# A decoder layer on one core: two left operands of the down projection's first group split in the feed-forward, and one set of copies given to ScalarE

## The chip, the core and the metric

The kernel runs on one core of a Trainium2 chip. The metric is device time in microseconds for one launch, median of three runs. All arithmetic is float32; a large matrix product is made of reduced-precision passes on TensorE, as told below.

## What is computed

One layer of a decoder with 1024 tokens and a model width of 1024. The change lies in the feed-forward (width 2816) and in its down projection; mixing and output projection stand ahead of them, a gated embedding and a last norm behind.

```python
h = rms_norm(x, mix_norm_g[i])
z = h @ w_in[i]
...
x = x + jnp.concatenate([y_nsa, y_conv, y_gla], axis=-1) @ w_out[i]
h = rms_norm(x, ffn_norm_g[i])
x = x + (jax.nn.silu(h @ ffn_w_gate[i]) * (h @ ffn_w_up[i])) @ ffn_w_down[i]
gate = jax.nn.sigmoid(rms_norm(x, ple_norm_g[i]) @ ple_w_gate[i])
x = x + (p[i] @ ple_w_proj[i]) * gate
...
return rms_norm(x, final_norm_g)
```

## The kernel before

**Split operands.** A float32 matrix enters TensorE as two halves: `split` lets ScalarE cast it to the reduced type (the high half, line 1040) and lets VectorE or GpSimd subtract that from the original (the low half, line 267). Each product then takes three matmuls: high by high, low by high, high by low. A split tile is named `op`; it has 128 partitions and two halves of 512 columns (512 KiB).

**Seven products for eight.** Gate, up and down projections are made of 2 by 2 blocks by a Strassen-Winograd scheme: seven block products and a number of block sums. The sums lie on VectorE and GpSimd.

**The feed-forward** walks over 11 pairs of hidden tiles, `c` = 0 to 10. A pair's gate and up weights (`w_g`, `w_u`) are loaded and split, multiplied (lines 1051 to 1053), and drained by `quarters`. The activation leaves in four blocks a11, a21, a12, a22, held in two tiles `sg`. Already here the block sums that the down projection will want as left operands are made: s5 = a21 + a22 and s6 = s5 - a11 in the tile `sa` (lines 1318 and 267), s3 in `ws`, and a21 = a11 - a21. All seven left operands go to device memory in `actd[c]`, unsplit, by SyncE's queue (lines 1322 to 1326).

**The down projection** takes the pairs in four groups (`DOWN`): 0, 1, 2, then 3, 4, 5, then 6, 7, 8, then 9, 10. A group makes its seven products in the order 5, 6, 3, 1, 7, 4, 2, each over all its pairs. `Down` loads a pair's two weight tiles (`w_d`, line 1355), left operands 5 and 6 (one load of 512 KiB from `actd`, line 1365) and operand 2 (`st`, line 1360). `operands(n)` loads the later left operands two at a time (3 and 1; 7 and 4), makes the right operand's block sum on VectorE and splits both sides. The matmuls are line 1436: 4 row tiles by 3 pairs by 3 passes, 36 for a product of the first group, about 924 in all. `drain` adds each finished bank to the residual `x2` (line 1345), which has come back from device memory as `x1d` (line 1421); product 1 of the first group is copied to the tile `xp` instead (line 1399).

**What sets the order.** The program is recorded once to plan SBUF: each tile is given one of 50 slots, and a tile waits until the last user of its slot's former tile is done (a DMA that reads that tile is such a user). Then a scheduler orders the instructions of each engine; each engine takes them strictly in that order. SyncE's queue issues all the loads and stores spoken of here, in order too, so a load stands behind any store ahead of it. There, the first group's loads and splits are mixed with the last feed-forward pair's work.

## Time and profile before

| | |
|---|---|
| median of three runs | 1401.75 us (1401.25 to 1402.43) |
| the profiled execution, its own time | 1404.31 us |
| its span, first to last instruction | 1402.5 us |
| TensorE busy (matmuls) | 1373.9 us, 98% |
| VectorE, ScalarE, GpSimd busy | 1030.6, 658.9, 554.5 us |
| feed-forward, lines 1051 to 1053 | from 638 to 1066 us of the span |
| down projection, line 1436 | from 1049.5 to 1280 us |

The span is what the trace shows; the profiled execution's own time lies 1.8 us above it. TensorE's share is an average: what an edit is worth is read where TensorE waits. In a row of the timeline a bracket gives how long the engine was idle just before, and what ended that. "SPq" is SyncE issuing a DMA; the transfer itself runs on.

### The profile page before, as it was taken

The numbers are of one execution on the slowest core, as the hardware profiler recorded it, in microseconds if no ns is written. First come the engines' busy times: TensorE is split into PE (matmuls) and PEld (weight loads), VectorE is DVE, ScalarE is ACT, GpSimd is POOL, SyncE is SP. The second block draws the span as 40 slices with busy tenths as digits, with TensorE's granted clock in tenths as the row PEclk, the third lists the DMA queues.
The fourth block names the chain that finished last, engine by engine and source line by source line (L and its number), as shares of the span: only waits on it lengthen the run. The fifth ranks groups of instructions, "written<-read, shape, count | busy, mean of one in ns | idle before, by whom it ended". The sixth has DMA issues, their size and how long they took to land.

```text
span 1402.5 us, 19415 instructions
## 1 busy us (share of the span) xinstructions
PE 1373.9 (98%) x7080; PEld 1163.3 (83%) x7080; DVE 1030.6 (73%) x1870; ACT 658.9 (47%) x1286; POOL 554.5 (40%) x592
## 2 busy tenths in 40 slices
PE   8999999999999998999999999999999999999997
PEld 6898777889999987888878888888888788888886
DVE  3897557558998885658786777777689989897533
ACT  7331422247887885536433334333345344444532
POOL 3761444347887863101465566556510000000111
PEclk9999999999999999999999999999999999999999
DMA  9201013400000012441333222233356743521111
GB/s 361 75 16 40 11 54 102 153 17 5 5 9 5 5 61 89 170 150 46 113 113 109 84 87 105 98 113 113 113 212 242 256 147 116 176 79 65 69 40 46
DMA packets 55743, 135.68 MB, mean 97 GB/s; under 512 B 5412, under 2 KB 10206, under 8 KB 55646
## 3 DMA queue, kind: packets, MB, share of 16 engines
q1 hardware_dynamic: 55502, 134.42, 27.5%
q8 instruction: 55, 0.90, 0.3%
q14 instruction: 42, 0.34, 0.1%
q10 hardware_dynamic: 144, 0.01, 0.0%
HBM read 102.68 MB, written 31.73 MB: 96 GB/s over the span
## 4 chain that ended last, share of the span: by engine, by line
PE 87%; DVE 6%; DMA 3%; ACT 1%; POOL 1%; issue 1%; SPq 0%; POOLq 0%; DVEq 0%; ACTq 0%
PE banks L1436 13%; PE banks L1053 8%; PE banks L1052 8%; PE banks L1051 8%; PE banks L371 3%; PE banks L967 3%; PE banks L368 3%; PE banks L372 3%; PE banks L1011 2%; PE banks L1012 2%; PE banks L907 2%; PE banks L1152 2%; PE banks L1153 2%; PE banks L1154 2%; PE banks L1488 2%; PE banks L1486 2%
## 5 line engine op out<-in xcount | busy, mean ns | idle before, releaser
L1053 PE MATMUL banks<-op 128*128 128x512 f32 x616 | 237.8, 390 | 1.3 <-DVE op L267 1.3
L1052 PE MATMUL banks<-op 128*128 128x512 f32 x616 | 238.6, 390 | 0.0
L1051 PE MATMUL banks<-op 128*128 128x512 f32 x616 | 235.9, 390 | 0.3 <-ACT cp L1126 0.3
L1436 PE MATMUL banks<-op 128*128 128x512 f32 x924 | 212.8, 392 | 3.3 <-ACT op L1040 2.6
L1436 PEld LDWEIGHTS banks<-op 128*128 128x128 f32 x924 | 174.3, 189 | 41.0 <-ACT op L1040 3.4
L1040 ACT CAST op<-nat 128x512 fp32r<-128x512 f32 x200 | 118.9, 620 | 177.8 <-DVE op L267 58.8
L267 DVE TENSOR_TENSOR op<-nat,op 128x512 fp32r<-128x512 f32 x196 | 152.5, 799 | 29.6 <-ACT op L1040 29.4
L301 POOL TENSOR_SCALAR rsr<-ss 128x1 f32<-128x1 f32 x16 | 5.9, 368 | 342.2 <-ACT sq L1455 264.4
L1053 PEld LDWEIGHTS banks<-op 128*128 128x128 f32 x616 | 115.6, 188 | 26.4 <-DVE op L267 2.2
L1051 PEld LDWEIGHTS banks<-op 128*128 128x128 f32 x616 | 115.6, 188 | 25.1 <-ACT cp L1126 0.7
L1052 PEld LDWEIGHTS banks<-op 128*128 128x128 f32 x616 | 115.6, 188 | 24.3 <-issue 0.5
L267 DVE TENSOR_TENSOR op<-ws,op 128x512 fp32r<-128x512 f32 x88 | 87.9, 1002 | 52.5 <-ACT op L1040 52.4
L922 POOL TENSOR_SCALAR p<-p,sums,gates 128x640 f32<-128x640 f32 (+7 forms) x128 | 100.4, 795 | 37.1 <-DVE sums L918 27.5
L913 ACT ACTIVATE p<-p,mn 128x640 f32<-128x640 f32 (+7 forms) x128 | 94.7, 742 | 10.2 <-DVE mn L910 10.1
L368 PE MATMUL banks<-hT,whi 128*128 128x512 f32 x208 | 84.2, 406 | 6.8 <-ACT hT L324 6.2
L1040 ACT CAST op<-ws 128x512 fp32r<-128x512 f32 x88 | 54.4, 622 | 76.9 <-PE banks L1053 45.6
L371 PE MATMUL banks<-hT,whi 128*128 128x512 f32 x208 | 83.7, 402 | 0.5 <-DVE hT L325 0.5
L372 PE MATMUL banks<-hT,wlo 128*128 128x512 f32 x208 | 82.5, 398 | 0.0
L967 PE MATMUL banks<-cst,p 128*128 128x128 f32 x448 | 71.8, 276 | 2.2 <-DVE pt L267 1.2
L907 PE MATMUL banks<-k,qst 128*128 128x512 f32 (+2 forms) x192 | 68.3, 362 | 1.4 <-POOL qst L267 0.9
L267 DVE TENSOR_TENSOR pt<-banks,pt 128x512 fp32r<-128x512 f32 (+1 forms) x114 | 64.2, 570 | 6.3 <-ACT pt L978 5.3
L1345 DVE TENSOR_TENSOR x<-banks,x 128x512 f32<-128x512 f32 x96 | 64.1, 681 | 6.4 <-PE banks L1436 6.0
(306 smaller groups left out, 3306.2 us busy)
## 6 DMA issues: line engine op xcount, KB each, us to landing
nat<-actd SPq DMA_DIRECT2D x33, 512.0 KB, 5.6
nat<-in_w_g SPq DMA_DIRECT2D x22, 512.0 KB, 3.3
nat<-in_w_u SPq DMA_DIRECT2D x22, 512.0 KB, 3.2
nat<-in_w_d SPq DMA_DIRECT2D x22, 512.0 KB, 5.3
nat<-in_w_t SPq DMA_DIRECT2D x13, 512.0 KB, 4.1
actd<-sg SPq DMA_DIRECT2D x22, 256.0 KB, 2.4
actd<-sa SPq DMA_DIRECT2D x11, 512.0 KB, 2.8
actd<-sg SPq DMA_DIRECT2D x11, 512.0 KB, 3.7
```

The lines of the kernel that those rows point to most:

```text
L267: return eng.tensor_tensor(out=o, in0=i0, in1=i1, op=ALU.subtract)
L368: r = mm(o, hi[:, w], x[:, 0, :], start=kt == 0, stop=False)
L371: mm(o, hi[:, w], x[:, 1, :], start=False, stop=False)
L372: mm(o, lo_[:, w], x[:, 0, :], start=False, stop=kt == KT - 1)
L907: mark("pe", mm(ps[:, :max(w, 256)], q, kdup[br][g][:, k], start=True, stop=False))
L922: nc.gpsimd.tensor_scalar(out=ps_out[br][:, :n], in0=ps_out[br][:, :n], scalar1=sums[:, br:br + 1], scalar2=gates[:, qb, 3 * head(h) + 1 + ...
L967: nc.tensor.transpose(ps[:, (2 * m + e) * P:(2 * m + e + 1) * P], blk(e, kb, br, ka), ident)
L1040: nc.scalar.copy(o[:, 0, :], src)
L1051: mm(ps, w[:, 0, c], x[k][:, 0, :], start=start and k == 0, stop=False, skip_group_check=True)
L1052: mm(ps, w[:, 0, c], x[k][:, 1, :], start=False, stop=False, skip_group_check=True)
L1053: mm(ps, w[:, 1, c], x[k][:, 0, :], start=False, stop=k == 3, skip_group_check=True)
L1436: mm(groups[g][t], r[:, v, c], l[:, u, :], start=start and (i, u, v) == (0, 0, 0), stop=i == len(ops) - 1 and u == 1, skip_group_check=True)
```

## The change

Three things change. For the pairs of the first group (`c` in 0, 1, 2) the feed-forward splits s5 and s6 as soon as they are made, and stores the two split tiles in a new device array `acts` (two stores of 512 KiB where one of 512 KiB was). The down projection's first group loads those split tiles ready for TensorE (two loads of 512 KiB where one was), and so neither casts nor subtracts for the left side of products 5 and 6. And the first group's product 1 is copied from its banks by ScalarE, not VectorE.

```diff
+    acts = dram.tile([len(DOWN[0]), 2, P, 2, 512], F32, name="acts")
...
-                nc.sync.dma_start(out=actd[c, 0:2].rearrange("i p j -> p i j"), in_=sa)
+                if c in DOWN[0]:
+                    for i, x in enumerate((s5, s6)):
+                        nc.sync.dma_start(out=acts[c, i], in_=f(split(x)))
+                else:
+                    nc.sync.dma_start(out=actd[c, 0:2].rearrange("i p j -> p i j"), in_=sa)
...
-            self.load(5, 6)
+            self.cut = {}
+            if c in DOWN[0]:
+                for i in range(2):
+                    self.cut[5 + i] = B("op", F32R, (P, 2, 512))
+                    nc.sync.dma_start(out=f(self.cut[5 + i]), in_=acts[c, i])
+            else:
+                self.load(5, 6)
...
-            return split(x.a.pop(n)), split({3: x.b22, 1: x.b11, 7: x.b12, 2: x.b21}.get(n, x.t))
+            return x.cut.pop(n) if n in x.cut else split(x.a.pop(n)), split({3: x.b22, 1: x.b11, 7: x.b12, 2: x.b21}.get(n, x.t))
...
-                nc.vector.tensor_copy(p, o)
+                nc.scalar.copy(p, o)
```

The slots and the scheduler's order move with it, from the first pair of the feed-forward on. Three places matter below. A tile's number differs between the two programs.

VectorE, where the feed-forward's last sums (`ws`, `sa`) meet the first group's operands, before: `op_9722` and `op_9730` are the left sides of product 3 for the group's second and third pair, `op_9733` is the third pair's right side, and `ws_9512` is the last pair's s3.

```order
L267 TENSOR_TENSOR ws_9512<-sg_9454,sa_9524 128x512
L267 TENSOR_TENSOR op_9956<-st_9540,op_9956 128x512
L267 TENSOR_TENSOR op_9722<-nat_9567,op_9722 128x512
L267 TENSOR_TENSOR op_9730<-nat_9576,op_9730 128x512
L267 TENSOR_TENSOR op_9959<-nat_9536,op_9959 128x512
L267 TENSOR_TENSOR op_9962<-st_9548,op_9962 128x512
L267 TENSOR_TENSOR op_9965<-nat_9544,op_9965 128x512
L267 TENSOR_TENSOR op_9733<-nat_9552,op_9733 128x512
```

And now, where `op_9740` is the third pair's left side of product 3 (the other sides of product 3 stand further ahead) and `ws_9534` is the last pair's s3:

```order
L267 TENSOR_TENSOR op_9845<-nat_9722,op_9845 128x512
L1350 TENSOR_TENSOR x2_9616<-banks_67,x2_9616 128x512
L1350 TENSOR_TENSOR x2_9617<-banks_67,x2_9617 128x512
L267 TENSOR_TENSOR op_9740<-nat_9598,op_9740 128x512
L267 TENSOR_TENSOR ws_9534<-sg_9476,sa_9546 128x512
L1350 TENSOR_TENSOR x2_9618<-banks_67,x2_9618 128x512
```

Counted from the tenth pair's s5 (`sa` from `sg`), the last piece of product 3 was VectorE's 103rd instruction and is now its 82nd: six low halves fewer stand ahead of it, and the scheduler has put others behind it. On TensorE the first matmul that needs that piece was the 184th after the first of line 1436 and is now the 147th.

SyncE, at the same time, before: `nat_9712`, `nat_9720` and `nat_9728` are the loads of left operands 7 and 4 for the three pairs.

```order
L1365 DMA nat_9712<-actd_2367 128x2x512
L1325 DMA actd_2367<-sg_9454 128x512
L1365 DMA nat_9720<-actd_2367 128x2x512
L1322 DMA actd_2367<-sa_9524 128x2x512
L1324 DMA actd_2367<-sg_9453 128x2x512
L1326 DMA actd_2367<-sg_9454 128x512
L1355 DMA nat_10014<-in_w_d 128x1024
L1355 DMA nat_10022<-in_w_d 128x1024
L1365 DMA nat_10056<-actd_2367 128x2x512
L1323 DMA actd_2367<-ws_9512 128x512
L1365 DMA nat_9728<-actd_2367 128x2x512
```

And now, where the same three are `nat_9722`, `nat_9730` and `nat_9738`:

```order
L1376 DMA nat_9722<-actd_2367 128x2x512
L1376 DMA nat_9730<-actd_2367 128x2x512
L1330 DMA actd_2367<-sg_9476 128x512
L1376 DMA nat_9738<-actd_2367 128x2x512
L1331 DMA actd_2367<-sg_9476 128x512
L1327 DMA actd_2367<-sa_9546 128x2x512
L1329 DMA actd_2367<-sg_9475 128x2x512
L1360 DMA nat_10024<-in_w_d 128x1024
L1328 DMA actd_2367<-ws_9534 128x512
```

The third load stood behind the store of the last pair's s3 (`ws`); now it stands ahead of four of the five stores.

ScalarE, at the end of the feed-forward's first pair, now (the waits are in brackets; `op_6768` and `op_6772` are the split s5 and s6, `op_6914` is the first weight operand of the next pair's up product):

```order
L1040 CAST op_6768<-sa_6763 128x512 [waits DVE_49]
L1040 CAST op_6772<-sa_6763 128x512 [waits DVE_49]
L1040 CAST op_6868<-ws_6812 128x512 [waits Pool_49]
L1116 COPY cp_6836<-banks_67 128x512 [waits PE_49]
L1040 CAST op_6930<-nat_6747 128x512 [waits DMAHW0_49,Activation_49]
L1040 CAST op_6850<-ws_6812 128x512 [waits DVE_49]
L1040 CAST op_6914<-nat_6747 128x512 [waits DMAHW5_49,Activation_49]
```

The first two casts are new. `op_6914` takes the slot of `op_6768`, so its cast waits for that tile's store; before, the same operand's cast waited for the store of `sa`. TensorE wants it at the 238th matmul of the feed-forward, before at the 250th.

## Rows read from the trace of the kernel before

**Rows 1.** The page, busy time by engine: busy us, share of the span, instructions.

```profile
PE 1373.9 (98%) x7080; PEld 1163.3 (83%) x7080; DVE 1030.6 (73%) x1870; ACT 658.9 (47%) x1286; POOL 554.5 (40%) x592
```

**Rows 2.** Stretches of 20 us: busy us (count) by engine, clock, DMA share, GB/s.

```profile
core 0: us, PE busy (x) PEld busy (x) DVE busy (x) ACT busy (x) POOL busy (x), PEclk, DMA share, GB/s
...
1060.00:1080.00 20.00, 20.00 (x90) 16.57 (x89) 19.76 (x34) 10.65 (x20) 0.00 (x0) 1.00 0.57 196
1080.00:1100.00 20.00, 16.67 (x68) 12.71 (x67) 19.52 (x33) 9.69 (x18) 0.00 (x0) 0.95 0.78 282
1100.00:1120.00 20.00, 20.00 (x87) 16.47 (x86) 18.74 (x32) 8.26 (x15) 0.00 (x0) 0.96 0.60 216
```

**Rows 3.** Timeline of TensorE, start of the down projection (start us, us, idle before).

```profile
1049.53 0.84 PE L1436 MATMUL banks<-op 128*128 128x512 f32 x3
...
1066.08 16.48 PE L1436 MATMUL banks<-op 128*128 128x512 f32 x72
1083.33 9.15 PE L1436 MATMUL banks<-op 128*128 128x512 f32 x39 [0.78 <-ACT op L1040]
1093.27 2.10 PE L1436 MATMUL banks<-op 128*128 128x512 f32 x8 [0.78 <-DVE op L267]
1097.14 13.02 PE L1436 MATMUL banks<-op 128*128 128x512 f32 x49 [1.77 <-ACT op L1040]
```

**Rows 4.** Short stretches of TensorE alone: busy us, clock, DMA.

```profile
1098.00:1100.00 2.00, 2.00 (x7) 0.53 1.04 410
1100.00:1104.00 4.00, 4.00 (x16) 0.81 0.89 331
```

**Rows 5.** Timeline of VectorE over the same time.

```profile
1029.01 0.69 DVE L1318 TENSOR_TENSOR sa<-sg 128x512 f32<-128x512 f32 x1
...
1070.89 0.68 DVE L1345 TENSOR_TENSOR x<-banks,x 128x512 f32<-128x512 f32 x1
...
1091.93 1.88 DVE L267 TENSOR_TENSOR op<-nat,op 128x512 fp32r<-128x512 f32 x3
```

**Rows 6.** Timelines of SyncE's issues and of ScalarE.

```profile
1050.85 12.11 SPq L1421 DMA_DIRECT2D x<-x1d  x16
...
1076.40 0.37 SPq L1365 DMA_DIRECT2D nat<-actd  x1
...
1089.81 0.42 SPq L1323 DMA_DIRECT2D actd<-ws  x1
1090.32 0.39 SPq L1365 DMA_DIRECT2D nat<-actd  x1
...
1096.47 1.14 ACT L1040 CAST op<-nat 128x512 fp32r<-128x512 f32 x2 [3.04 <-DMA nat<-actd]
```

**Rows 7.** DMA rate from 1020 to 1120 us, in 40 slices of 2.5 us.

```profile
GB/s 0 3 0 105 7 298 345 307 395 413 402 388 396 391 387 386 387 388 308 272 2 0 2 207 332 193 134 264 123 392 414 405 391 146 0 51 359 327 211 243
```

**Rows 8.** Feed-forward's first pairs: TensorE's waits, a cast, landings of the `sa` store.

```profile
704.16 0.50 PE L1053 MATMUL banks<-op 128*128 128x512 f32 x1 [0.78 <-DVE op L267]
...
711.96 0.50 PE L1051 MATMUL banks<-op 128*128 128x512 f32 x1 [0.26 <-ACT cp L1126]
...
734.31 0.50 PE L1053 MATMUL banks<-op 128*128 128x512 f32 x1 [0.52 <-DVE op L267]
...
696.79 0.62 ACT L1040 CAST op<-nat 128x512 fp32r<-128x512 f32 x1 [8.08 <-DMA actd<-sa]
...
DMA to landing us min/median/max: 2.8/2.8/6.6
```

**Rows 9.** A stretch of 20 us there, columns as in rows 2.

```profile
700.00:720.00 20.00, 18.97 (x82) 14.92 (x81) 17.57 (x18) 8.94 (x15) 13.89 (x10) 1.00 0.15 54
```

**Rows 10.** Groups by line and shape: busy us, mean ns (the last from 600 to 740).

```profile
L1040 ACT CAST op<-nat 128x512 fp32r<-128x512 f32 x117 | 68.2, 619 | 80.7 <-PE banks L1436 40.4 <-DVE op L267 19.3 <-DMA nat<-actd 10.8
...
L1399 DVE COPY xp<-banks 128x512 f32<-128x512 f32 x4 | 2.6, 678 | 0.0
...
L1095 ACT COPY cp<-banks 128x512 f32<-128x512 f32 x3 | 1.7, 580 | 7.7 <-PE banks L1053 7.7
...
L267 DVE TENSOR_TENSOR op<-nat,op 128x512 fp32r<-128x512 f32 x19 | 17.8, 953 | 6.6 <-ACT op L1040 6.5
```

## Prediction

> **What bounds the kernel now.** I read the busy times first: TensorE is at 98% of the span [rows 1], so an edit elsewhere can only give back time in which TensorE stands or runs slowly. Next I read its list of waits and the same engine over stretches. In the feed-forward's steady part and from 1120 us on it never stands. Around the change it stands in two places: three times in the first group of the down projection [rows 3], and three times briefly in the feed-forward's first pairs [rows 8].
>
> The first place is the dear one. Idle time there is 0.78 + 0.78 + 1.77 = 3.33 us [rows 3], and behind it the granted clock is 0.53 for 2 us and 0.81 for 4 us [rows 4]; before, the clock was full [rows 2]. Undisturbed matmuls start (16.48 - 0.39) / 71 = 0.2266 us apart (0.39 us being one matmul, 72 of them in the row) [rows 3]. The two disturbed stretches hold 68 and 87 matmuls where an undisturbed one holds 90, that is 25 too few [rows 2], and 25 by 0.2266 is 5.7 us. Clock and idle time alone give 3.33 + 2 x 0.47 + 4 x 0.19 = 5.0 us. So 5.0 to 5.7 us lie there, and I take 5.6.
>
> Why does it stand? VectorE is busy 19.5 to 19.8 us of each 20 there [rows 2], with one instruction of 128x512 every 0.602 us (three take 1.88 us with the last one's 0.68) [rows 5]. It is a backlog: the last pair's sums and the first group's low halves share one queue. Count it. The last low half of product 3 is instruction 103 after the sum at 1029.01 us; 103 x 0.602 is 62.0 us, so 1091.0 us, and with some waits on the way it is the second in the row of 1091.93 us, ready at about 1093.2 [rows 5]. TensorE would want it at 1049.53 + 184 x 0.2266 = 1091.2 us [rows 3]: 2 us late, the first two waits. The third wait has another cause: a cast at 1096.47 us waited for a load issued at 1090.32 us, right behind the store of `ws` at 1089.81 us [rows 6], which needs VectorE's sum of the last pair. That is the backlog again, by way of SyncE's order.
>
> **The change, part by part.** *Work taken from the crowded stretch.* Six casts and six low halves go. On ScalarE, busy about half of that time [rows 2], six casts of 0.62 us are worth nothing by themselves. On VectorE six instructions are 3.6 us. With the new order, the last piece of product 3 is instruction 82: 1029.01 + 82 x 0.602 = 1078.4 us, with 1 us of waits as now and its own 0.68 ready at 1080.1. TensorE wants it at 1049.53 + 147 x 0.2266 = 1082.8 us. From 2 us late it becomes 2.7 us early. The last operand of product 7 was wanted 192 matmuls in, at 1093.0 us, and came at 1097.1 [rows 3]; it is now wanted 222 in, at 1099.8 us, as VectorE's instruction 106, ready at about 1094.5. Its load no longer stands behind the store of `ws`, and its slot comes free 63 instructions in, at 1067 to 1068 us; behind the residual's loads it should land before 1080. I credit the whole 5.6 us and then charge what follows.
>
> *Loads added.* Three more loads of 512 KiB, 1.57 MB, enter a stretch in which DMA runs at 386 to 413 GB/s from 1040 to 1065 us [rows 7]: 4.0 us of transfer. Everything behind them is up to 4.0 us later. The residual's sixteen loads, last issued at 1050.85 + 12.11 = 1063 us [rows 6] and moved by about 1068 [rows 7], then end at about 1072. The first drains, at 1070.89 us now [rows 5], need only the earlier ten of them, 1.5 MB sooner, so by about 1068; the rest are wanted by product 6's drains, some 80 instructions in, at about 1077. The third pair's weights are wanted by VectorE 44 instructions in, 1055.5 us, and may come 0.5 to 1.5 us after that. That wait eats into the 2.7 us margin. Bounds: 0 (inside the margin) and 4.0 - 2.7 = 1.3 us with a fall of the clock as now, 1.7 us, so 3.0. I charge 0.5, since the margin is nearer to covering it.
>
> *Product 1's copies.* Four instructions of 0.68 us leave VectorE and four of 0.58 us enter ScalarE [rows 10]. Before, they lie at about 1105 us, where TensorE runs at work in hand [rows 2]; product 2, which adds to the same banks, starts 20 matmuls or 4.5 us after product 1 ends. Cost and gain nothing, unless ScalarE stands then (second rival).
>
> *Splits added to the feed-forward.* At the end of pairs 0, 1 and 2, two casts of 0.62 us and two low halves of about 0.95 us (that is their mean there, beside GpSimd's work) [rows 10]. ScalarE is busy 8.9 and VectorE 17.6 of 20 us in the fullest stretch [rows 9]; over a pair's 38 us there is room. From both sides: the 1.56 us that TensorE stands there now could vanish, or all six low halves could be exposed, 6 x 0.95 = 5.7 us. I take 0, nearer the first, as VectorE has idle time in every such stretch.
>
> *The store that holds a slot.* Now the next pair's operand waits for the store of `sa`; its cast starts at 696.79 us after 8.08 us of idle ScalarE, and the low halves behind it are late by the 0.78 us at 704.16 [rows 8]. After the change the operand waits for the store of split s5 and is wanted 12 matmuls earlier, 2.7 us. TensorE's want was about 697.5 us (the cast just met it); it becomes 694.8. With an issue at about 690 us and landings of 2.8 to 6.6 us [rows 8], the cast would end between 693.4 and 697.2: 1.4 us early to 2.4 late. I take 0, since the median landing of the eleven stores is 2.8 us, the least of them. The Trainium skill, in "DMA: Bandwidth & Descriptors", section "Anatomy of one DMA", speaks against splitting into more stores: each DMA has a fixed part of about 2 us, most of it the receipt of the write, plus its bytes by 436 GB/s. For 512 KiB that is an estimate of 3.2 us a store by that page, fitted to another engine's DMAs; with it the cast would end 1.0 us early and the charge stays 0, while the slowest landing of the trace would cost 2.4 us a pair.
>
> Sum: -5.6 + 0.5 + 0 + 0 = -5.1 us. Of the profiled execution's 1404.31 us that makes 1399.2; it was 2.6 us longer than the median of 1401.75, and against that median the forecast is **1396.6 us**.
>
> **The rivals.** *Second: the hole moves.* For it speaks the DMA rate, at its ceiling already [rows 7], and that ScalarE's new order puts a cast for the next group, whose load must wait for a slot until about 1094 us, ahead of the third pair's left operand of product 2, which TensorE wants 246 matmuls in, at 1105.3 us. Against it: either has about 3 us of room. If the 4.0 us appear in full, 3.0 us come back in place of 0.5: 1401.75 - 5.6 + 3.0 = 1399.2; with worse landings up to 1401.
>
> *Third: no effect.* If the waits come from SyncE's queue and the slots alone and not from VectorE's backlog, the loads land as late as now: 1401.5 us. For it speaks the third wait, which ended with a DMA [rows 6]; against it, that the store ahead of that load waited for VectorE.
>
> *Fourth: slower.* The stores of split tiles hold slots in the first three pairs. At the slowest landing, 2.4 us a pair is 7.2 us, and one fall of the clock adds 1.7: 1401.75 - 5.1 + 8.9 = 1405.5 us. It decides from (5.1 + 2.8 - 1.7) / 3 = 2.1 us a pair. For it: TensorE already stands three times just there [rows 8]. Against: 2.8 us is the median landing, and 6.6 us the worst [rows 8].
>
> **How the numbers follow.** The likeliest case has 0.66; its own range is 1394.5 (5.7 us back and the 1.56 us too) to 1398.5. The second has 0.16, the third 0.10, the fourth 0.08. Beyond 0.2% of 1401.75, 2.8 us, a measurement of this kernel tells a change from none. All of the first and some 0.06 of the second lie below 1398.9: faster 0.72. Same is 0.10 of the second and the third, 0.20; slower 0.08. For 8 in 10 the range runs from 1394.5 to 1401.0, which takes in the second case and leaves out the third and fourth.
>
> **What would show it.** Right: TensorE's three waits of rows 3 are gone or under 0.5 us in sum, the stretches up to 40 us behind the first line 1436 matmul (now 1447) hold 90 matmuls each at full clock, and the feed-forward's first pairs wait no more than 1.6 us in all. Loads added: the residual's loads end about 4 us later with VectorE short of a drain for 1 us at most. Wrong: a wait of TensorE on a cast or low half near 1080 to 1105 us with a clock below 1 behind it (second), the third load of operands 7 and 4 still issued near 1090 us (third), or waits of 2 us and more near 695, 735 and 773 us that end with a cast held by a DMA from `acts` (fourth).

## Result and the profile after

The changed kernel takes **1418.2 us** (median of five runs, 1414.5 to 1422.0) against 1402.4 us for the kernel before (1401.3 to 1407.9): a ratio of 1.011, 95% interval 1.0089 to 1.013. It is 1.1% slower where 0.4% faster was forecast, and far outside the range.

The profiled execution took 1419.36 us, its span 1417.6 us. The page's busy times, which answer to [rows 1], hardly move: TensorE 5 us more, VectorE 6 us more.

```profile
PE 1379.2 (97%) x7080; PEld 1164.3 (82%) x7080; DVE 1036.8 (73%) x1866; ACT 662.7 (47%) x1290; POOL 554.9 (39%) x592
```

The loss is found by stages. The summary of TensorE's lines gives the first and last start of a line's matmuls: 1051 is the feed-forward's first pass, 1447 (before: 1436) the down projection. First the kernel before, then the changed one:

```profile
L1051 PE MATMUL banks<-op x616: 387/389/799, 638.0 to 1065.4; 128*128 128x512 f32 x154
...
L1436 PE MATMUL banks<-op x924: 387/389/628, 1049.5 to 1279.8; 128*128 128x512 f32 x185
```

```profile
L1051 PE MATMUL banks<-op x616: 387/389/799, 640.0 to 1083.5; 128*128 128x512 f32 x154
...
L1447 PE MATMUL banks<-op x924: 387/389/502, 1067.9 to 1295.4; 128*128 128x512 f32 x185
```

From the first matmul of the feed-forward to the first of the down projection it is 1067.9 - 640.0 = 427.9 us; before, 1049.5 - 638.0 = 411.5. From there to the end of the last one of the down projection (0.4 us long) it is 227.9 us; before, 230.7. So in this profile 2.8 us came back where 5.6 were credited, and 16.4 us were lost where nothing was expected. Below these two lengths are called the feed-forward and the down projection. (The 2 us ahead of 640 us are not read as an effect of the change: in the runs below that keep the 46 slots the first matmul of the feed-forward lies anywhere from 633.5 to 642.1 us.)

Stretches of 20 us, columns as in [rows 2]:

```profile
680.00:700.00 20.00, 19.06 (x85) 15.34 (x84) 19.16 (x27) 8.05 (x14) 9.50 (x5) 1.00 0.47 169
...
740.00:760.00 20.00, 16.93 (x67) 13.76 (x68) 10.89 (x14) 8.60 (x14) 6.52 (x6) 0.91 0.24 89
...
780.00:800.00 20.00, 15.80 (x63) 12.51 (x62) 13.50 (x15) 7.22 (x12) 9.93 (x7) 0.91 0.40 143
1080.00:1100.00 20.00, 20.00 (x90) 16.57 (x89) 20.00 (x35) 10.68 (x20) 0.00 (x0) 1.00 0.88 320
1100.00:1120.00 20.00, 18.51 (x81) 14.69 (x81) 18.44 (x31) 7.67 (x14) 0.00 (x0) 1.00 0.76 281
```

Two feed-forward stretches hold 67 and 63 matmuls of 90, and none of the engines beside TensorE is full there. In the whole feed-forward TensorE now stands 12.7 us in eight waits, before 1.6 us in three. Its longest waits there, and in the first group of the down projection:

```profile
743.07 0.50 PE L1051 MATMUL banks<-op 128*128 128x512 f32 x1 [3.92 <-ACT op L1040]
...
788.32 0.50 PE L1051 MATMUL banks<-op 128*128 128x512 f32 x1 [4.20 <-ACT op L1040]
...
1110.31 16.87 PE L1447 MATMUL banks<-op 128*128 128x512 f32 x72 [1.49 <-ACT op L1040]
1127.89 12.31 PE L1447 MATMUL banks<-op 128*128 128x512 f32 x53 [0.71 <-DVE x L1350]
```

The last two answer to [rows 3]: 2.2 us in place of 3.33, and the clock behind them stays at 1.00. The first two, 8.1 of the 12.7 us, are new. Who was late? ScalarE's timeline at the first of them:

```profile
734.31 0.59 ACT L1126 COPY cp<-banks 128x512 f32<-128x512 f32 x1
740.93 1.06 ACT L1308 ACTIVATE sg<-sg 128x1024 f32<-128x1024 f32 x1 [6.03 <-DVE sg L1272]
741.90 0.60 ACT L1040 CAST op<-ws 128x512 fp32r<-128x512 f32 x1
742.40 0.61 ACT L1040 CAST op<-nat 128x512 fp32r<-128x512 f32 x1
```

ScalarE stood 6 us in front of a Silu of the next pair's gate; the cast that TensorE wants is queued behind it. The Silu waits for VectorE, where the pair's sums and the split's two low halves (`op<-sa`) stand ahead of the gate's quarters (lines 1271 and 1272):

```profile
734.56 0.68 DVE L267 TENSOR_TENSOR op<-sa,op 128x512 fp32r<-128x512 f32 x1
735.16 1.77 DVE L267 TENSOR_TENSOR ws<-sg,sa 128x512 f32<-128x512 f32 x1
736.85 0.68 DVE L267 TENSOR_TENSOR op<-nat,op 128x512 fp32r<-128x512 f32 x1
737.46 1.77 DVE L267 TENSOR_TENSOR op<-sa,op 128x512 fp32r<-128x512 f32 x1
739.15 0.68 DVE L1271 TENSOR_TENSOR sg<-banks,cp 128x512 f32<-128x512 f32 x1
739.86 1.04 DVE L1272 TENSOR_TENSOR sg<-sg,rbc 128x512 f32<-128x512 f32 x1
```

And on GpSimd the sum behind the wanted cast (`ws<-nat`, line 1105) was itself late, by 0.87 us for a slot that a store still read; it was done at 738.68 us, 3.2 us ahead of its cast:

```profile
729.40 1.68 POOL L1314 TENSOR_TENSOR sg<-cp,sg 128x512 f32<-128x512 f32 x1 [0.63 <-DVE cp L1272]
734.98 1.41 POOL L1136 TENSOR_TENSOR cp<-cp 128x512 f32<-128x512 f32 x1 [3.90 <-ACT cp L1126]
737.26 1.42 POOL L1105 TENSOR_TENSOR ws<-nat 128x512 f32<-128x512 f32 x1 [0.87 <-DMA actd<-sg]
```

Before, GpSimd did the same pair's two products of gate and up (line 1313) together, at 721.74 us, and had the next sum at 730.70:

```profile
721.74 2.93 POOL L1313 TENSOR_TENSOR sg<-cp,sg 128x512 f32<-128x512 f32 x2 [0.63 <-DVE cp L1271]
729.01 1.29 POOL L1136 TENSOR_TENSOR cp<-cp 128x512 f32<-128x512 f32 x1 [4.34 <-ACT cp L1126]
730.70 1.30 POOL L1105 TENSOR_TENSOR ws<-nat 128x512 f32<-128x512 f32 x1 [0.39 <-PE banks L1053]
```

So the second product ended 4.4 us later than before (731.08 against 724.67, less the 2 us of the start), since the scheduler had moved it behind other work. The theories to part: **work** (twelve casts and low halves in the way), **stores** (a second store of 512 KiB a pair, and slots held until it lands; the prediction's fourth rival), **order** (of the engines' queues), and, as none of the first three explained all of it, **slots** (each split tile takes one of the 46 slots of 4 KiB per partition).

### The profile page after: what moved, and what is told of

Read it like the earlier page. It is cut to its first block, busy times and chain, and to the rows that moved or that the text cites. A ratio compares the mean times of both kernels' runs of the same rounds, so it can differ in the third digit from the quotient of the medians.

```text
span 1417.6 us, 19465 instructions
## 1 busy us (share of the span) xinstructions
PE 1379.2 (97%) x7080; PEld 1164.3 (82%) x7080; DVE 1036.8 (73%) x1866; ACT 662.7 (47%) x1290; POOL 554.9 (39%) x592
## 4 chain that ended last, share of the span: by engine, by line
PE 85%; DVE 7%; POOL 3%; ACT 2%; DMA 2%; issue 2%; SPq 0%; POOLq 0%; DVEq 0%; ACTq 0%
PE banks L1447 13%; PE banks L1051 7%; PE banks L1053 7%; PE banks L1052 7%; PE banks L371 3%; PE banks L368 3%; PE banks L372 3%; PE banks L967 3%; PE banks L1011 2%; PE banks L1012 2%; DVE op L267 2%; PE banks L907 2%; PE banks L1153 2%; PE banks L1154 2%; PE banks L1498 2%; PE banks L1497 2%
## 5 line engine op out<-in xcount | busy, mean ns | idle before, releaser
L1040 ACT CAST op<-nat 128x512 fp32r<-128x512 f32 x194 | 115.3, 621 | 144.5 <-DVE op L267 58.8
L267 DVE TENSOR_TENSOR op<-nat,op 128x512 fp32r<-128x512 f32 x190 | 147.1, 799 | 29.7 <-ACT op L1040 29.3
L267 DVE TENSOR_TENSOR op<-ws,op 128x512 fp32r<-128x512 f32 x88 | 85.0, 970 | 52.3 <-ACT op L1040 52.1
```

The source lines that it names most:

```text
L267: return eng.tensor_tensor(out=o, in0=i0, in1=i1, op=ALU.subtract)
L1040: nc.scalar.copy(o[:, 0, :], src)
```

## The experiments

Each was run beside the kernel before on one chip; ratios are to that kernel. The lengths are those of each profile (before: 411.5, 427.4 and 230.7 us). "To its last" is the feed-forward from the first to the last start of its first pass (line 1051, in f2, f4 and f5 line 1052). It is needed because the border moves: in e8, f3, f4, f5 and the two g2 runs ten to twelve more feed-forward matmuls stand behind the down projection's first one than in the kernel before, 2.3 to 2.7 us at 0.2266 us each, so that the feed-forward comes out that much too short and the down projection too long.

| run | median us | ratio (95%) | feed-forward | to its last | down projection |
|---|---|---|---|---|---|
| changed | 1418.2 | 1.0089 to 1.0130 | 427.9 | 443.5 | 227.9 |
| e3_ffn_half | 1417.7 | 1.0084 to 1.0137 | 428.8 | 444.6 | 227.2 |
| e4_down_half | 1400.5 | 0.9977 to 1.0001 | 412.0 | 427.6 | 228.1 |
| e1_copy_only | 1403.7 | 0.9995 to 1.0025 | 411.7 | 427.6 | 228.4 |
| e5_work_no_store | 1408.9 | 1.0029 to 1.0060 | 421.5 | 437.4 | 228.5 |
| e6_store_no_work | 1400.0 | 0.9966 to 1.0001 | 413.3 | 428.9 | 226.9 |
| e10_order_only | 1413.3 | 1.0063 to 1.0117 | 425.3 | 441.2 | 228.9 |
| e12_same_order | 1420.2 | 1.0094 to 1.0147 | 427.3 | 443.1 | 228.9 |
| e8_split_later | 1407.6 | 1.0020 to 1.0054 | 417.7 | 435.6 | 228.9 |
| e11_sums_first | 1406.7 | 1.0016 to 1.0048 | 419.1 | 434.8 | 228.1 |
| f3_later_two | 1407.8 | 1.0021 to 1.0053 | 413.3 | 431.2 | 231.7 |
| e13_old_order | 1417.4 | 1.0082 to 1.0123 | 427.7 | 443.4 | 227.3 |
| e14_five_old | 1416.3 | 1.0081 to 1.0125 | 414.1 | 429.7 | 239.3 |
| f2_silu_behind | 1412.5 | 1.0040 to 1.0086 | 425.7 | 441.4 | 227.3 |
| f4_low_behind | 1415.7 | 1.0071 to 1.0129 | 426.9 | 444.8 | 229.4 |
| f5_both_orders | 1418.2 | 1.0089 to 1.0139 | 427.1 | 445.0 | 228.9 |
| g2_slots45 | 1413.2 | 1.0041 to 1.0085 | 409.8 | 428.4 | 233.8 |
| g2_slots44 | 1433.1 | 1.0186 to 1.0233 | 423.2 | 442.0 | 233.2 |
| g3_one_slot | 1400.1 | 0.9953 to 0.9980 | 410.6 | 426.2 | 227.9 |

### Which half of the change

**e3_ffn_half**, against the changed kernel:

```diff
-                for i in range(2):
-                    self.cut[5 + i] = B("op", F32R, (P, 2, 512))
-                    nc.sync.dma_start(out=f(self.cut[5 + i]), in_=acts[c, i])
+                w = B("nat", F32, (P, 2, 512))
+                nc.sync.dma_start(out=w, in_=acts[c, :, :, 0, :].rearrange("i p j -> p i j"))
+                self.a[5], self.a[6] = w[:, 0, :], w[:, 1, :]
...
-                nc.scalar.copy(p, o)
+                nc.vector.tensor_copy(p, o)
```

> Only the feed-forward's half of the change: the split tiles are made and stored as in the changed kernel, but the down projection reads their rounded halves (one load of two tiles) and splits them again itself, as before, and product 1 is copied by VectorE. The low halves of these two operands are left out of the result. If the loss comes from the feed-forward (order, stores or work, no matter which): that stage, from its first matmul to the down projection's first, takes about 428 us as in the changed kernel (411.5 before), and the whole about 1402.4 + 16 = 1418 us. If the loss came from the three added loads or from the copy by ScalarE: about 1402 us and a feed-forward of 411.5 us.

It has the whole loss: feed-forward 428.8 us.

**e4_down_half**, against the changed kernel:

```diff
+    for c in range(3):
+        for i in range(2):
+            nc.sync.dma_start(out=acts[c, i], in_=f(xop[c][i]))
...
-                if c in DOWN[0]:
-                    for i, x in enumerate((s5, s6)):
-                        nc.sync.dma_start(out=acts[c, i], in_=f(split(x)))
-                else:
-                    nc.sync.dma_start(out=actd[c, 0:2].rearrange("i p j -> p i j"), in_=sa)
+                nc.sync.dma_start(out=actd[c, 0:2].rearrange("i p j -> p i j"), in_=sa)
```

> Only the down projection's half: the feed-forward stores unsplit as before, the first group loads split tiles for its first two products (six stores of tiles of the output projection fill them earlier, so these two products' left operands are other data), product 1 is copied by ScalarE. By the prediction's credit the transition gives 5.1 us back: 1402.4 - 5.1 = 1397.3 us. By the trace of the changed kernel it gives 2.8 us: 1399.6 us. The feed-forward stays at 411.5 us in both.

The down projection's half by itself gives 0.11% back, 1.5 us, in an interval from 3.2 us to nothing: it leaves out the prediction's 5.1, and a gain at all is not clear of noise.

**e1_copy_only**, against the kernel before:

```diff
-                nc.vector.tensor_copy(p, o)
+                nc.scalar.copy(p, o)
```

> The kernel before with only product 1's four copies of the first group moved to ScalarE. The feed-forward's order is unchanged on every engine. By the prediction the copies are worth nothing: 1402.5 us within 1.5, the down projection's waits of 3.3 us as before. If the copies were what shortens the transition in the changed kernel: waits of about 2.2 us there and 1399 to 1400 us.

No difference that can be measured, as forecast; the waits at the transition are 3.8 us, against 3.33 in the kernel before. But the clock is another there:

```profile
PE banks L1436 <- ACT op L1040: 2.2, 2, 1.4
PE banks L1436 <- DVE op L267: 1.6, 2, 0.8
...
1080.00:1100.00 20.00, 17.02 (x73) 13.15 (x72) 19.81 (x34) 9.07 (x17) 0.00 (x0) 1.00 0.81 288
1100.00:1120.00 20.00, 20.00 (x90) 16.57 (x89) 18.69 (x32) 10.88 (x20) 0.00 (x0) 1.00 0.62 226
```

The kernel before shows 0.95 and 0.96 in these two stretches [rows 2]. In e5, e10 and e12, whose down projection is also the old one, TensorE waits 2.7 to 3.2 us there, the clock is 1.00, and the down projection takes 228.5 to 228.9 us. So about 2 us of the 230.7 are a fall of the clock that one trace of the kernel before shows and four kernels with the same transition do not. Against these four, the changed kernel's 227.9 us is a gain of 0.5 to 1.0 us, about what its shorter waits give (3.33 - 2.2 = 1.1).

### Work or stores

**e5_work_no_store**: the splits are made, nothing of them is stored or loaded, product 1 is copied by VectorE.

```diff
-                if c in DOWN[0]:
-                    for i, x in enumerate((s5, s6)):
-                        nc.sync.dma_start(out=acts[c, i], in_=f(split(x)))
-                else:
-                    nc.sync.dma_start(out=actd[c, 0:2].rearrange("i p j -> p i j"), in_=sa)
+                nc.sync.dma_start(out=actd[c, 0:2].rearrange("i p j -> p i j"), in_=sa)
+                if c in DOWN[0]:
+                    for x in (s5, s6):
+                        split(x)
```

> The changed kernel's two splits at the ends of pairs 0 to 2, but nothing of them is stored: the tile of both sums is stored unsplit as before, the first group loads it as before, VectorE copies product 1. So the twelve added instructions without the added stores and loads. GpSimd's order is a third one (both products of gate and up behind the next pair's second sum). If the work or the order that comes with it costs the time: feed-forward 420 to 428 us, whole 1411 to 1419 us. If the stores that hold slots cost it: 411 to 413 us and 1402 us.

**e6_store_no_work**: the bytes without the splits.

```diff
-                    for i, x in enumerate((s5, s6)):
-                        nc.sync.dma_start(out=acts[c, i], in_=f(split(x)))
+                    for i in range(2):
+                        nc.sync.dma_start(out=acts[c, i], in_=sa)
```

> The changed kernel with its two stores of 512 KiB a pair, its loads and its copies by ScalarE, but without the twelve casts and low halves: each store writes the unsplit tile of both sums (so the left operands of the first group's first two products are other data). GpSimd's order is mixed: products of gate and up apart in pair 0, together in pairs 1 and 2 as before. If the stores' bytes and slots cost the time: feed-forward 420 us and more, whole over 1409 us. If work and order do it: feed-forward 411 to 415 us, whole 1399 to 1402 us.

Two stores a pair cost at most 1.8 us in three pairs; the splits without stores cost 10. So the bytes and the second issue are not the loss. A split tile whose slot is held by its store is in neither run: in e6 both stores read `sa`, and in e5 no store reads the split tiles. The 6.4 us between e5 and the changed kernel can be that, or the other order that comes with it; no run parts the two.

### Order

A dependency without a semaphore holds an instruction behind another in the scheduler's order and adds no instruction. **e10_order_only** (kernel before; `behind` adds such a dependency on the last marked instruction):

```diff
+                    if i == 1 and c in DOWN[0]:
+                        mark("pool", ins)
...
-            self.eng.tensor_tensor(out=self.s, in0=self.a21, in1=self.a22, op=ALU.add)
+            ins = self.eng.tensor_tensor(out=self.s, in0=self.a21, in1=self.a22, op=ALU.add)
+            behind("pool", ins)
```

> The kernel before, with nothing added but an order: on GpSimd, in the pairs whose successors follow pairs 0 to 2, the next pair's first sum may not stand ahead of the first product of gate and up of this pair. No split, no store, no copy moved. If the order opens the holes: a feed-forward longer by 5 to 20 us, with TensorE waiting 3 us and more near 743 and 788 us for a cast, and the whole between 1407 and 1422 us. If the added work or stores do it: 1402 us within 2.

Feed-forward 425.3 us: moving one sum behind one product on GpSimd, in three pairs, costs 13.8 us. The long waits are others than forecast, 1.54 and 2.17 us each near 726 and 771 us.

**e12_same_order** goes on from there with four more such dependencies, so that GpSimd has the changed kernel's order in pairs 0 to 2 (but for one place):

```diff
+            before(held6, sub(self.eng, self.s, self.s, self.a11))
...
+            mark("sum", self.sum)
+            behind("sum", ins)
+            before(heldb, ins)
...
+            before(held, ins)
```

> The kernel before with GpSimd's instructions of pairs 0 to 2 held in the order that they have in the changed kernel (the first product of gate and up ahead of the next pair's first sum, the second behind that pair's last sum). Nothing added, no split, no store, no copy. If that order opens the holes: the feed-forward takes 420 us and more (411.5 before, 427.9 changed), with TensorE's long waits for a cast at 740 to 745 and 780 to 790 us, and the whole 1411 to 1418 us. If the splits' work or their stores are needed for it: feed-forward 411 to 414 us, whole 1402 us within 2.

With nothing added to it the kernel before loses as much as by the change: feed-forward 427.3 us. Its long waits lie elsewhere, 3.5 us at 698.9 and 0.9 + 1.5 us each near 738 and 782, all for casts or low halves. So a bad order suffices, without a slot more. Does a good one cure? **e8_split_later** writes the splits behind the next pair's Silu:

```diff
-                    for i, x in enumerate((s5, s6)):
-                        nc.sync.dma_start(out=acts[c, i], in_=f(split(x)))
+                    held = c, s5, s6
...
+                if held:
+                    for i, x in enumerate(held[1:]):
+                        nc.sync.dma_start(out=acts[held[0], i], in_=f(split(x)))
+                    held = None
```

> The changed kernel, with the two splits and their two stores written one place later in the program: behind the Silu of the next pair's gate tiles instead of at the end of their own pair. Same instructions, same bytes; on GpSimd the order of the feed-forward is nearly that of the kernel before (the next pair's first sum stands ahead of the products of gate and up). If the order of instructions opened the holes: the feed-forward is back at 411 to 414 us and the whole at 1399 to 1402 us. If the two stores' slots or the twelve added instructions cost the time by themselves: both are still there, the feed-forward stays over 420 us and the whole over 1410 us.

**e11_sums_first** brings the next pair's sums forward:

```diff
+                nx = pair(c + 1, 0)
+                if nx and nx.w5 is None and c in DOWN[0]:
+                    nx.sums()
```

> The changed kernel with all its instructions, stores and loads, but the next pair's first sum and split are written ahead of this pair's products of gate and up, for pairs 0 to 2. GpSimd then does both products of gate and up behind one another and ahead of the next pair's last sum, nearly as before. If the order costs the time: feed-forward 411 to 418 us, whole 1399 to 1407 us. If work or stores do it, wherever they stand: feed-forward 420 us and more, whole over 1410 us.

Both win back about half, not all: to its last matmul the feed-forward takes 435.6 and 434.8 us, between 427.4 and 443.5. In e8 the long waits of pairs 1 and 2 are gone; one is left behind pair 0, where a slot is held by the store of a split tile (GpSimd's and TensorE's timelines of e8):

```profile
701.49 1.29 POOL L1105 TENSOR_TENSOR ws<-nat 128x512 f32<-128x512 f32 x1 [4.81 <-DMA acts<-op]
...
709.69 0.78 PE L1053 MATMUL banks<-op 128*128 128x512 f32 x1 [2.02 <-DVE op L267]
```

**f3_later_two** is e8 with pair 0 left unsplit (`c in (1, 2)` for `c in DOWN[0]`).

> As the run with the later split, but pair 0 is stored and loaded unsplit, so that the one long hole of that run (5.4 us near 710 us, behind GpSimd's sum that waited 4.8 us for a store of a split tile) should be gone. Two thirds of the added work stay. If that store's slot was what remained: feed-forward 411 to 413.5 us and a whole of 1399 to 1402 us. If the added instructions cost by their number: feed-forward 415 to 417 us, whole 1403 to 1406 us.

Feed-forward 413.3 us, but that is short by ten matmuls: to its last one it is 431.2, 3.8 us more than before. Of these, 2.3 us are six waits of 0.38 or 0.39 us from 808 us on, in pairs where nothing is split: the edit moves the order there too. So pair 0's hole is gone, and the two pairs that still split have no wait over 0.5 us. (The whole, 1407.8 us, is above the expectation: the down projection, which now loads one pair unsplit, has a wait of 2.9 us.)

### One link at a time

These undo parts of the order in the changed kernel itself. **e13_old_order** holds GpSimd to the order of before in pairs 0 and 1 (in pair 2 the two products part again):

```diff
+            before(held3, sub(self.eng, self.s3, self.a11, self.a21))
...
+            before(held, ins)
```

> The changed kernel with nothing left out, but GpSimd held to the order of the kernel before through pairs 0 to 2 (both products of gate and up behind the next pair's last sum). The twelve added instructions, the stores and the loads are all there. If GpSimd's order is the whole of the loss: feed-forward 411 to 414 us and, with 1 to 3 us back in the down projection, a whole of 1399 to 1402 us. If the added instructions on VectorE and ScalarE cost as well, as the feed-forwards of 417.7 to 421.5 us in the runs with another order let one suspect: feed-forward 416 to 421 us, whole 1404 to 1409 us.

**f2_silu_behind** moves the Silu behind the cast of the up tile's first sum, **f4_low_behind** the two low halves behind the gate's first quarters, **f5_both_orders** is e13 and f4 together:

```diff
+            for ins in held:
+                tc.add_manual_dep(ins.ins, casts[-1].ins.name,
+                                  mybir.DependencyInfo(mybir.DependencyClass.NoSync, mybir.DependencyReason.DATA))
...
+        before(heldv, mult(nc.vector, c12, c12, rr[1]))
```

> The changed kernel with one pair of instructions moved on ScalarE: the Silu of the next pair's first gate tile, after pairs 0 to 2, may not stand ahead of the cast of that pair's first up sum. Order of TensorE and GpSimd as changed. In the changed kernel that sum was ready at 738.7 us and its cast stood behind the Silu until 742.5 us. If the Silu's place in ScalarE's queue makes the hole: the waits of 3.9 and 4.2 us for a cast shrink to 0.7 us each, with up to 2 us left for the low half on VectorE (free at 740.9 us); feed-forward 421 to 425 us in place of 427.9. If VectorE's lateness or GpSimd's order decides and the Silu only stood in the way by chance: feed-forward 426 to 429 us.

> The changed kernel with the two low halves of the split held behind the next pair's first gate quarters on VectorE (0.68 + 1.77 us of work that stood ahead of them). If VectorE's queue at the pair's end makes the hole: Silu and cast come 2.45 us sooner, the two long holes shrink to 1.5 to 2 us, feed-forward 421 to 424 us. If GpSimd's order alone decides, which stays as changed but for the place of one product: 426 to 429 us.

> The changed kernel, nothing left out, with two orders held together: GpSimd as in the kernel before through pairs 0 to 2, and VectorE's low halves of the split behind the next pair's first gate quarters. Each alone brought little back (feed-forward 427.7 and 426.9 us). If the loss is the order and only its links lie side by side, so that one held link leaves the others: feed-forward 413 to 419 us, whole 1400 to 1408 us, like the run in which the splits were written later. If something else in the changed kernel costs the time: feed-forward 424 us and more, whole over 1412 us.

My theory of order fell here as far as a cure goes. To its last matmul, where the changed kernel takes 443.5 us, the feed-forward gets back 0.1 us by GpSimd's old order and 2.1 by the Silu (less than expected: the two waits shrink only to 2.41 and 3.72); with the low halves moved it takes 1.3 us more, and with the first two together 1.5 more. In f5 the longest wait lies in pair 0, and a slot stands at its start: GpSimd's sum waits for a store that reads the slot, the cast for the sum, and behind the cast in ScalarE's queue stands the copy that frees TensorE's bank (GpSimd, ScalarE twice, TensorE of f5):

```profile
693.38 1.26 POOL L1113 TENSOR_TENSOR ws<-nat 128x512 f32<-128x512 f32 x1 [3.23 <-DMA actd<-sg]
...
695.89 0.62 ACT L1041 CAST op<-ws 128x512 fp32r<-128x512 f32 x1 [3.01 <-POOL ws L267]
696.42 0.58 ACT L1144 COPY cp<-banks 128x512 f32<-128x512 f32 x1
...
697.05 0.50 PE L1052 MATMUL banks<-op 128*128 128x512 f32 x1 [4.07 <-ACT cp L1144]
```

**e14_five_old** is e13 with the split of product 5's operand alone, so with one split tile a pair:

```diff
-                    for i, x in enumerate((s5, s6)):
-                        nc.sync.dma_start(out=acts[c, i], in_=f(split(x)))
+                    nc.sync.dma_start(out=acts[c, 0], in_=f(split(s5)))
+                    nc.sync.dma_start(out=actd[c, 1], in_=s6)
```

> As the run with the old order, but only the operand of product 5 is split in the feed-forward; that of product 6 is stored and loaded unsplit as before. Half of the added instructions (three casts, three low halves). If order is all: feed-forward 411 to 414 us, whole 1399 to 1402 us, like the run with both. If the instructions cost by their number: about half of what the run with both loses in the feed-forward, 414 to 416 us, and a whole of 1401 to 1404 us.

Feed-forward 414.1 us: with one tile a pair 2.6 us are lost, with two 16 (in this run half of the casts and low halves is gone too). Its whole time is lost elsewhere: product 6's operand now has a tile of its own in the down projection, and a wait of 7.6 us at 1092.8 us goes with it.

### Slots

**g2_slots45** and **g2_slots44** are the kernel before with fewer slots:

```diff
-SLOTS = {1024: 1, 2048: 2, 3072: 1, 4096: 46}
+SLOTS = {1024: 1, 2048: 2, 3072: 1, 4096: 44}
```

> The same with 45 slots. If held slots cost the time: between the run with 44 and the kernel before, feed-forward 418 to 445 us. If not: 411 to 416 us.

> The kernel before, unchanged but for the number of its 4 KiB slots of on-chip memory: 44 in place of 46, all through the program. No split, no added store, no copy moved. The changed kernel holds two such slots more at the end of pairs 0 to 2, for the two split tiles. With 44 slots GpSimd's order in the feed-forward becomes that of the changed kernel, and it is so in all pairs, not in three. If the two held slots are what opens the holes: about 16.4 / 3 = 5.5 us a pair, so a feed-forward of 440 to 470 us (411.5 before), with TensorE's waits of about 4 us for a cast in each pair, and a whole of 1435 to 1470 us. If the twelve added instructions or the added stores are needed: feed-forward 411 to 416 us.

```profile
L1051 PE MATMUL banks<-op x616: 387/389/799, 648.1 to 1090.1; 128*128 128x512 f32 x154
```

With two slots fewer, and no other edit, the scheduler gives GpSimd the changed kernel's order in the feed-forward, and to its last matmul that stage takes 442.0 us (the line above), 14.6 more; by the other length, which is short by twelve matmuls here, 11.7 more. With one fewer it is 428.4, a loss of 1.0. So the direction was right and the size was not (440 to 470 expected of the first length, which is 423.2). The loss has another shape than the changed kernel's: TensorE stands 7.8 us in fifteen waits spread over the stage, the longest 1.23 us at 700.9 and 1.80 us at 1064.5; the two waits of 4 us are not there. (Both kernels lose outside the feed-forward too, since their slots are short everywhere: from the start to its first matmul 645.7 and 648.1 us against 638.0.)

**g3_one_slot**, against the changed kernel, makes the same twelve instructions and stores the same bytes, but takes one slot more than the kernel before in place of two:

```diff
-                    for i, x in enumerate((s5, s6)):
-                        nc.sync.dma_start(out=acts[c, i], in_=f(split(x)))
+                    o = B("op", F32R, (P, 2, 512))
+                    for i, x in enumerate((s5, s6)):
+                        nc.scalar.copy(o[:, i, :], x)
+                        sub(nc.vector, x.bitcast(F32R), x, f(o[:, i, :]))
+                    for u, x in enumerate((f(o), sa)):
+                        nc.sync.dma_start(out=acts[c, :, :, u, :].rearrange("i p j -> p i j"), in_=x)
```

> The changed kernel with the same twelve instructions and the same stored bytes, but one slot more instead of two: the two rounded halves go to one tile, and the low halves are written over the sums themselves. If the held slots are the cause: feed-forward 415 to 422 us (427.9 with two slots), whole 1402 to 1411 us. If the work, the stores or their place in the program cost it: 426 to 429 us, whole 1416 to 1419 us.

The feed-forward is back at 410.6 us, better than expected, and the whole at **1400.1 us** against 1404.6 us for the kernel before in the same set of runs: 0.34% faster (interval 0.20% to 0.47%). It beats both kernels. All of TensorE's waits from 640 us to the end of the down projection, from its list of waits:

```profile
PE banks L1051 <- ACT cp L1095: 0.5, 1, 0.5
PE banks L1053 <- DVE op L267: 0.5, 1, 0.5
...
PE banks L1451 <- ACT op L1040: 1.5, 1, 1.5
PE banks L1451 <- DVE x L1354: 0.4, 1, 0.4
```

The last two are those of the changed kernel, 1.9 us against 2.2. And neither the work nor the time that the stores take can have been the cause by itself: the instructions are the same here, ScalarE even waits longer for the stores than in the changed kernel (8.5 us against 3.0), and they land no sooner. From issue to landing, first the changed kernel, then g3:

```profile
DMA to landing us min/median/max: 3.1/4.8/7.4
```

```profile
DMA to landing us min/median/max: 3.7/4.9/6.8
```

## Why the prediction was wrong

**What bounds the kernel.** The waits at the transition were read rightly as the place to win: they fell from 3.33 to 2.2 us. The fall of the clock behind them [rows 4] was not: it stands in the one trace that the prediction had, and not in e1, e5, e10 and e12, which wait there as long.

**Work taken from the crowded stretch, credit 5.6 us: mis-sized.** The profile shows 2.8 us, but about 2 of these are that fall of the clock; e4 gives 1.5 us, not clear of nothing, and against the four kernels named it is 0.5 to 1.0 us. Two things were too large: the 2.3 us of the credit that were clock, and the hope that all waits end. The backlog was shortened, not ended: VectorE is busy 20.00 of 20 us from 1080 to 1100 still, and the wait of 1.49 us at 1110.3 is for a cast, whose engine had stood 4.27 us for VectorE's low halves. I had counted the distance of one operand of product 3 and one of product 7, and not that of the others in the same queue.

**Loads added, 0.5 us: right in size.** The residual's loads were issued until 17.4 us behind the down projection's first matmul, before until 13.4, which is the 4 us forecast. The one wait for a drain's sum is 0.71 us; that these loads made it is not shown, since just before it VectorE stood 3.19 us for casts, and ScalarE 2.77 us for a load of a later operand.

**Product 1's copies, nothing: right** (e1).

**Splits added to the feed-forward, "I take 0, nearer the first, as VectorE has idle time in every such stretch": this is the step that failed.** It cost 16.4 us, outside the bounds of -1.56 and 5.7, which were both made of engine time. Busy time was not what ran short. What did is seen from two sides, the slots: with the same instructions and bytes and one slot less the loss is gone (g3), and with two slots less and no instruction the kernel before loses 14.6 us in the same stage, with one less 1.0 (g2). Why two and not one is the limit, the runs do not show. The way from the slots to the waits is argued and not shown: the order alone makes the same loss (e12), undoing links one by one leaves the others (e13, f2, f4, f5), and with the slots alone changed the order changes too and the waits are others (g2_slots44). So how much of the 16.4 us is order and how much is waiting for a slot stays open. g3 differs from the changed kernel in three more points, its order, the place of its low halves and the shape of its two stores; the order follows from the slots in g2_slots44, the other two were not tried by themselves.

**The store that holds a slot, 0: the mechanism exists, the size was nearly right.** The cast named there waited 2.77 us for a store from `acts`, and TensorE lost 0.94 us at 696.9 us, inside the bounds of 1.4 early to 2.4 late. The stores landed after 4.8 us in the median, not the 2.8 taken. The two long waits near 743 and 788 us end otherwise, and e6 bounds the price of the second store's bytes at 1.8 us for three pairs. So the fourth rival was right in its sign and in naming held slots, and wrong in the way by which they cost: it priced the landing of one store, 2.4 us a pair, less than half of the 16.4 / 3 = 5.5 measured. 0.08 was too little for a case whose price I had made of one wait.

**What would show it.** Waits of 2 us and more near 735 and 773 us were the sign written down for the fourth rival; they came at 743 and 788, and without the DMA that was to end them.

## What to carry to other kernels

Before work is moved to an earlier stage, count the tiles that it keeps alive there and not only its engine time: in a full on-chip memory one more tile cost nothing here and two cost 16 us. If the count goes up, look for a form that writes into a tile already held, as the low halves over their sums do here. And where a scheduler makes the order, compare the order of all engines at the place that receives the work, since it moves for instructions that were not edited.

## What the runs showed of the hardware

**VectorE beside GpSimd.** The same subtraction `op<-sa,op` of 128x512 took 0.68 us at 734.56 us, ahead of GpSimd's sum, and 1.77 us at 737.46 us, begun 0.2 us behind a sum of 1.42 us on GpSimd (737.26 us). The Trainium skill, "SBUF — State Buffer", section "Summary: rules for kernel authors", says that VectorE with two inputs from SBUF and a GpSimd operation that reads SBUF block each other, the second until the first is done; the trace agrees. So moving GpSimd's work in time moves VectorE's prices too.

**The clock falls behind some waits.** The stretches with a wait of about 4 us have a granted clock of 0.91, so part of them ran at the lower level of 1.2 GHz; in g3, with no wait over 0.6 us in the feed-forward, it is 1.00. A wait does not bring it each time: a stretch with a wait of 2.90 us has 0.91 in f3 (1080 to 1100 us), and one with a wait of 2.93 us has 1.00 in e14 (760 to 780 us); the waits of 1.77 us before and 1.4 to 1.6 us in e1, e10 and e12 at the same place have 0.95 and 1.00. So a loss to the clock that one trace shows is not yet a gain to be had. Between runs of one kernel the mean clock moves as well: of twelve runs of e8 the fastest, 1402.7 us, had 0.996, and the slowest, 1412.3 us, 0.990. Differences of 2 us need many runs for that reason.
